# Rotary embedding in place, 32 KB rows: stores moved from SyncE's DMA ring to ScalarE's, one more load in advance

## The chip, the cores and the metric

One core of one Trainium2 chip. The metric is the device time of one execution in microseconds (us), as a median of three or more executions. The profile's span is about 1.8 us shorter than that time.

Words used below. *PE* is TensorE, *DVE* VectorE, *ACT* ScalarE, *SP* SyncE. A *DMA engine* is one of the core's 16 engines that move data; a *ring* is the queue of descriptors that one issuing engine fills, with a part on each of the 16. A *packet* is one record of the trace of a DMA engine's work. *Load n* and *store n* are the transfers of slab n, 0 to 7.

## The reference, cut to what matters

```python
# x: (16, 512, 1024) fp32; cos, sin: (512, 32) fp32; 16 heads of 64
x = x.reshape(batch, seq, num_heads, head_dim)
x1, x2 = x[..., :half_dim], x[..., half_dim:]
rotated = concatenate([x1 * cos - x2 * sin,
                       x1 * sin + x2 * cos], axis=-1)
```

33.6 MB are read and 33.6 MB written, and there is little arithmetic for each byte.

## The kernel before

A slab is two batches: 4 MB, 128 partitions with one contiguous row of 32 KB each. The slab is loaded, worked on in place in four chunks of 2,048 columns, and stored from the same tile. There are eight slabs and five slots for them. For each chunk ACT casts to bf16, DVE multiplies by the cosine and by the signed sine table, PE adds the two products (the second with its halves swapped) through an identity matrix into PSUM, and ACT copies the sum back into the slab.

```python
nb = 2; slots = 5; lead = 4; rows = 2        # W = 8192, PW = 2048 columns

def load(s):
    slab[s] = slabs.tile([P, W], f32, tag="slab", name="slab")
    nc.sync.dma_start(out=slab[s], in_=dram(x, s))

for s in range(lead):
    load(s)
# ... cos and sin are loaded in ScalarE's ring; tables are built ...
for s in range(nslabs):
    xs = slab.pop(s)
    for k in range(rpp // rows):
        # ... xb = bf16(xk); t1 = xb * cc; t2 = xb * ss; acc = t1 + swap(t2) ...
        nc.scalar.copy(out=xk, in_=acc)
    nc.sync.dma_start(out=dram(out_flat, s), in_=xs)
    if s + lead < nslabs:
        load(s + lead)
```

## Time and profile before

| | before |
|---|---|
| median time, three runs | 164.93 us (164.80 to 165.01) |
| span of the profile | 163.1 us |
| mean rate over the span | 412 GB/s |
| share of the 16 DMA engines' time, ring q1 | 96.3% |
| ACT busy | 117.3 us (72%) |

From the page of the kernel before: ACT's and the DMA's row (the span in 40 slices, busy share in tenths), then the rings with packets, MB and share of the 16 engines' time.

```profile
ACT  3006648999899999998997999999789999100000
...
DMA  6999998999999999999999999999999999999980
...
q1 hardware_dynamic: 2304, 67.11, 96.3%
q10 hardware_dynamic: 160, 0.13, 0.2%
q8 instruction: 2, 0.03, 0.1%
q14 instruction: 2, 0.02, 0.0%
HBM read 33.69 MB, written 33.55 MB: 412 GB/s over the span
```

The DMA row is full from end to end, and ACT, the busiest compute engine, stops one seventh of the span early. The stores are issued at 34.2 to 139.1 us (the view of their line):

```profile
L133 SPq DMA_DIRECT2D out_dram<-slab x8: 332/344/378, 34.2 to 139.1; - x8
```

So the DMA engines bound this kernel. All data is in q1, SyncE's ring; q10, ScalarE's, holds the two tables. The two lines called "instruction" are four small transfers that fetch the kernel's own instructions.

The next view is the last microseconds, in windows of 1 us; the columns of use here are the last two, the share of the DMA engines and GB/s. The view counts a packet in the window in which it starts, so a full window can read over 1.00, and an engine at work on one 32 KB packet (1.2 us) can show nothing.

```profile
157.00:158.00 1.00, 0.00 (x0) 0.00 (x0) 0.00 (x0) 0.00 (x0) 0.00 (x0) 0.50 1.06 459
158.00:159.00 1.00, 0.00 (x0) 0.00 (x0) 0.00 (x0) 0.00 (x0) 0.00 (x0) 0.50 0.31 131
159.00:160.00 1.00, 0.00 (x0) 0.00 (x0) 0.00 (x0) 0.00 (x0) 0.00 (x0) 0.50 0.08 33
160.00:161.00 1.00, 0.00 (x0) 0.00 (x0) 0.00 (x0) 0.00 (x0) 0.00 (x0) 0.50 0.08 33
161.00:162.00 1.00, 0.00 (x0) 0.00 (x0) 0.00 (x0) 0.00 (x0) 0.00 (x0) 0.50 0.00 0
```

A packet is 1.21 us of one engine, 1.21 / 16 = 0.076 of the 16. So 0.08 is exactly one engine: from 159 us on, single engines start a last packet while the others are done. The individual records say the same: most engines end between 158.3 and 159.4 us, two at 160.0 and 160.1, and the last at 161.8.

The chain of work that ended last, by engine, follows the compute and never names a store:

```profile
PE 28%; ACT 24%; issue 14%; DMA 10%; DVE 8%; ACTq 0%; DVEq 0%
```

### The profile page before, as it was taken

The numbers are of one execution on the slowest core, as the hardware profiler recorded it, in microseconds if no ns is written. First come the engines' busy times: TensorE is split into PE (matmuls) and PEld (weight loads), VectorE is DVE, ScalarE is ACT, GpSimd is POOL, SyncE is SP. The second block draws the span as 40 slices with busy tenths as digits, with TensorE's granted clock in tenths as the row PEclk, the third lists the DMA queues.
The fourth block names the chain that finished last, engine by engine and source line by source line (L and its number), as shares of the span: only waits on it lengthen the run. The fifth ranks groups of instructions, "written<-read, shape, count | busy, mean of one in ns | idle before, by whom it ended". The sixth has DMA issues, their size and how long they took to land.

```text
span 163.1 us, 830 instructions
## 1 busy us (share of the span) xinstructions
PE 78.8 (48%) x258; PEld 28.8 (18%) x258; DVE 76.0 (47%) x69; ACT 117.3 (72%) x65; POOL 1.1 (1%) x8
## 2 busy tenths in 40 slices
PE   0001189458918863974199419905990696000000
PEld 0000024112402320331033103301330132000000
DVE  0001699079537755871597069609920991000000
ACT  3006648999899999998997999999789999100000
POOL 2000000000000000000000000000000000000000
PEclk9999999985795997599858956995597599855555
DMA  6999998999999999999999999999999999999980
GB/s 225 426 394 402 466 434 386 466 434 402 482 402 402 498 382 410 482 396 426 450 410 444 442 410 426 450 418 442 426 426 438 426 426 450 418 450 418 434 370 16
DMA packets 2468, 67.29 MB, mean 412 GB/s; under 512 B 288, under 2 KB 416, under 8 KB 416
## 3 DMA queue, kind: packets, MB, share of 16 engines
q1 hardware_dynamic: 2304, 67.11, 96.3%
q10 hardware_dynamic: 160, 0.13, 0.2%
q8 instruction: 2, 0.03, 0.1%
q14 instruction: 2, 0.02, 0.0%
HBM read 33.69 MB, written 33.55 MB: 412 GB/s over the span
## 4 chain that ended last, share of the span: by engine, by line
PE 28%; ACT 24%; issue 14%; DMA 10%; DVE 8%; ACTq 0%; DVEq 0%
PE acc L127 15%; ACT slab L132 15%; PE acc L125 13%; DMA sin_sb<-in_sin_dram 10%; ACT xb L115 10%; DVE t L121 7%; DVE t L120 1%; PE acc L104 0%; ACTq L77 0%; DVE ss L94 0%; DVE ss L96 0%; ACTq L132 0%; DVEq L120 0%; DVE ss L106 0%; ACTq L115 0%
## 5 line engine op out<-in xcount | busy, mean ns | idle before, releaser
L125 PE MATMUL acc<-t,ident 128*128 128x512 bf16 x128 | 59.1, 462 | 34.3 <-DVE t L120 31.0
L115 ACT CAST xb<-slab 128x2048 bf16<-128x2048 f32 x32 | 59.2, 1904 | 13.0 <-DMA slab<-in_x_dram 10.4
L132 ACT COPY slab<-acc 128x2048 f32<-128x2048 f32 x32 | 58.9, 1869 | 6.9 <-PE acc L127 6.7
L127 PE MATMUL acc<-t,ident 128*128 128x512 bf16 x128 | 58.3, 455 | 6.6 <-DVE t L121 6.6
L120 DVE TENSOR_TENSOR t<-xb,cc 128x2048 bf16<-128x2048 bf16 x32 | 39.1, 1221 | 42.1 <-ACT xb L115 42.1
L121 DVE TENSOR_TENSOR t<-xb,ss 128x2048 bf16<-128x2048 bf16 x32 | 39.0, 1219 | 0.0
L127 PEld LDWEIGHTS <-ident 128*128 128x128 bf16 x128 | 14.4, 112 | 56.5 <-issue 48.5
L125 PEld LDWEIGHTS <-ident 128*128 128x128 bf16 x128 | 14.2, 111 | 38.7 <-issue 27.7
L104 PE MATMUL acc<-cc,spread 64*128 64x512 bf16 x1 | 0.6, 582 | 12.7 <-DVE cc L91 12.7
L91 DVE CAST cc<-cos_sb 64x512 bf16<-64x512 f32 x1 | 0.4, 419 | 12.3 <-DMA cos_sb<-in_cos_dram 12.3
L104 PE MATMUL acc<-ss,spread 64*128 64x512 bf16 x1 | 0.6, 583 | 4.7 <-DVE ss L96 4.7
L115 ACT ACT_TABLE_LOAD x1 | 1.3, 1283 | 1.9 <-issue 1.9
L94 DVE CAST ss<-sin_sb 64x256 bf16<-64x256 f32 x1 | 0.3, 285 | 4.8 <-DMA sin_sb<-in_sin_dram 4.8
L104 PEld LDWEIGHTS <-spread 64*128 64x128 bf16 x2 | 0.2, 102 | 12.6 <-issue 10.8
L106 DVE CAST ss<-acc 128x512 bf16<-128x512 f32 x1 | 0.7, 692 | 0.1
L106 DVE CAST cc<-acc 128x512 bf16<-128x512 f32 x1 | 0.7, 676 | 0.0
L85 POOL COPY spread<-ident 64x64 bf16<-64x64 bf16 x2 | 0.4, 230 | 0.1
masks.py:199 POOL TENSOR_SCALAR_AFFINE_SELECT ident<-ident 128x128 bf16<-128x128 bf16 x1 | 0.3, 292 | 0.1
L96 DVE TENSOR_SCALAR ss<-sin_sb 64x256 bf16<-64x256 f32 x1 | 0.3, 278 | 0.0
masks.py:197 POOL MEMSET ident<- 128x128 bf16 x1 | 0.2, 205 | 0.3 <-POOLq L152 0.3
L152 POOL MEMSET const-bfloat16-1.0<- 128x1 bf16 x1 | 0.1, 101 | 0.0
L152 POOL MEMSET const-uint8-127<- 128x1 uint8 x1 | 0.1, 101 | 0.0
(2 smaller groups left out, 0.2 us busy)
## 6 DMA issues: line engine op xcount, KB each, us to landing
slab<-in_x_dram SPq DMA_DIRECT2D x8, 4096.0 KB, 30.2
out_dram<-slab SPq DMA_DIRECT2D x8, 4096.0 KB, 28.9
cos_sb<-in_cos_dram ACTq DMA_DIRECT2D x1, 64.0 KB, 11.5
sin_sb<-in_sin_dram ACTq DMA_DIRECT2D x1, 64.0 KB, 16.2
```

The lines of the kernel that those rows point to most:

```text
L85: nc.gpsimd.tensor_copy(out=spread[:, g * SP:(g + 1) * SP], in_=ident[:SP, :SP])
L91: nc.vector.tensor_copy(out=cc1, in_=view(cos_sb, 0, (half, rpp), (0, 2), (1, half)))
L94: nc.vector.tensor_copy(out=view(ss1, 0, (hd, rpp), (1, half)), in_=sin_rows)
L96: nc.vector.tensor_scalar_mul(out=view(ss1, half, (hd, rpp), (1, half)), in0=sin_rows, scalar1=-1.0)
L104: nc.tensor.matmul(view(acc, q, (1, n)), spread, view(one, q, (1, n)), start=True, stop=True)
L106: nc.vector.tensor_copy(out=wide, in_=view(acc, 0, (1, rpp * hd)))
L115: nc.scalar.copy(out=xb, in_=xk)
L120: nc.vector.tensor_mul(out=t1, in0=xb, in1=tab(cc))
L121: nc.vector.tensor_mul(out=t2, in0=xb, in1=tab(ss))
L125: nc.tensor.matmul(bank, ident, view(t1, q, (1, BANK)), start=True, stop=False)
L127: nc.tensor.matmul(bank, ident, view(t2, q + half, (hd, hpb), (-half, 2), (1, half)), start=False, stop=True)
L132: nc.scalar.copy(out=xk, in_=acc)
```

## The change

The intent: loads in SyncE's hardware ring and stores in ScalarE's, so that the DMA engines alternate between the two by packet.

```diff
-    lead = 4
+    lead = 5
@@
-        nc.sync.dma_start(out=dram(out_flat, s), in_=xs)
+        nc.scalar.dma_start(out=dram(out_flat, s), in_=xs)
         if s + lead < nslabs:
             load(s + lead)
```

## The prediction

> **What bounds the kernel now.** The 16 DMA engines. The page's DMA row reads 9 of 10 almost throughout, and the queue section gives ring q1 96.3% of all engines' time. The trace's packet records: the 67.1 MB are 2,048 packets of 32,768 B, 128 per engine; nearly all take 1,213 ns and start as the one before ends (1,209 ns apart). 128 x 1.21 = 155 us; first packets start at 1.8 to 2.7 us; most engines end at 158.3 to 159.4 us, the slowest at 161.8; the span is 163.1. No engine idles for want of work. Compute is hidden: in the timeline ScalarE runs from 13.6 to 139.1 us, 117 us busy; the last 22 us are stores alone.
>
> **What the change does.** It removes no byte. Loads stay in SyncE's ring; stores go to ScalarE's. The Trainium skill ("DMA: Bandwidth & Descriptors", section "Queues, rings and completion order") says that each engine goes round-robin between rings by packet. The trace agrees: the cos and sin loads in ScalarE's ring, four 1 KB packets per engine each, alternate with 32 KB load packets. So a load and a store in flight each get half the rate, where now they take turns of 9.7 us.
>
> Loads 0 to 4 are queued at once instead of 0 to 3; loads 5, 6, 7 still wait for stores 0, 1, 2. I expect store 0 issued at about 34 us (as now) and done at 54 to 56 (now 52.9), and loads 5, 6, 7 to land near 87, 106 and 126 us (now 81.9, 101.4, 120.8).
>
> **The new dependence.** ScalarE's program order, compared with the one before, holds eight DMA issues, each after the next slab's first casts: store 6 stands behind two casts and a copy of slab 7, so it waits for load 7. Each issue costs ScalarE about 0.4 us (SyncE's take 0.33 to 0.40), 3 us in all, hidden. But slab 7 lands 5 us later. With casts of 1.9, two DVE products of 1.22, eight matmuls in 1.7 to 3.4 and copies of 1.87 us, I estimate store 6's issue at 134 to 136 and store 7's at 147 to 149 us (before: 139.1). A store takes 9.7 us alone, so store 7 must be issued by about 148 us or the engines run dry: the slack shrinks to nothing, costing 0 to 3 us.
>
> **A cost per switch.** By position in the slab, a load's last packet before a store takes 10 to 80 ns more on average; a store's last before a load some 10. With some 38 alternations per engine between 34 and 126 us that is an estimated 0 to 2 us. I see no gain: packets are already back to back at 27 GB/s per engine. A luckier slowest engine could give back 1 to 2 us.
>
> **Time.** 164.9 + about 1: 166.0 us, range 164.2 to 168.8. Faster by over 2%: 0.03; within 2%: 0.80; slower by over 2%: 0.17.
>
> **What would show it.** Right: about half of the DMA time each in q1 and q10, sum near 96%; packets still 1,213 to 1,250 ns; loads 5 to 7 landing 4 to 6 us later; ScalarE's last copy near 147 us; a full DMA row but for a dent near 145. Wrong: packets shorter or overlapping (gain), or longer than 1,260 ns (loss by alternation); ScalarE waiting for loads before slab 6; a hole before store 7.
>
> **What would break it.** Unfair arbitration between rings that delays load 7 or starves stores; a real cost or gain of mixing directions; PE at its lower clock in the last slab.

## The result, and the profile after

| | before | after |
|---|---|---|
| median of four runs | 164.87 us (164.68 to 165.01) | 163.49 us (163.27 to 163.78) |
| ratio | | 0.9918, 95% interval 0.9897 to 0.9939 |
| span of the profile | 163.1 us | 161.5 us |
| mean rate over the span | 412 GB/s | 416 GB/s |

A ratio is the mean time of one kernel's runs over that of the kernel before's runs of the same rounds, so it is not quite the ratio of the medians. Executions over 1.5% slower than the fastest of the same kernel are left out of the means. The change gains 0.8%, which is small and clear of the noise. The prediction forecast a loss of 1 us; the measured time lies under its range.

From the page after, the same rows:

```profile
ACT  3006647994999999899989998969990697918000
...
DMA  7999999999999999999999999999999999997996
...
q1 hardware_dynamic: 1152, 33.55, 48.9%
q10 hardware_dynamic: 1312, 33.69, 48.4%
q8 instruction: 2, 0.03, 0.1%
q14 instruction: 2, 0.02, 0.0%
HBM read 33.69 MB, written 33.55 MB: 416 GB/s over the span
```

Half of the data is in each ring. ACT now works to the end and has a hole before it; the DMA row has a dent (the 7, near 148 us). ACT's last instructions in order of time (start, duration, what, and the idle time before it with its releaser):

```profile
126.57 1.90 ACT L115 CAST xb<-slab 128x2048 bf16<-128x2048 f32 x1 [5.11 <-DMA slab<-in_x_dram]
...
134.16 0.34 ACTq L133 DMA_DIRECT2D out_dram<-slab  x1
...
145.80 3.63 ACT L132 COPY slab<-acc 128x2048 f32<-128x2048 f32 x2 [3.79 <-PE acc L127]
149.46 0.34 ACTq L133 DMA_DIRECT2D out_dram<-slab  x1
```

ACT waits 5.1 us for load 7, issues store 6 at 134.2 us and the last store at 149.5 us. This is too late to keep the DMA engines busy, as the windows of 1 us show:

```profile
147.00:148.00 1.00, 0.43 (x3) 0.00 (x0) 0.00 (x0) 1.00 (x2) 0.00 (x0) 1.00 1.14 492
148.00:149.00 1.00, 0.00 (x0) 0.00 (x0) 0.00 (x0) 1.00 (x1) 0.00 (x0) 1.00 0.23 98
149.00:150.00 1.00, 0.00 (x0) 0.00 (x0) 0.00 (x0) 0.43 (x1) 0.00 (x0) 1.00 0.08 33
150.00:151.00 1.00, 0.00 (x0) 0.00 (x0) 0.00 (x0) 0.00 (x0) 0.00 (x0) 1.00 1.22 524
...
158.00:159.00 1.00, 0.00 (x0) 0.00 (x0) 0.00 (x0) 0.00 (x0) 0.00 (x0) 0.50 1.22 524
159.00:160.00 1.00, 0.00 (x0) 0.00 (x0) 0.00 (x0) 0.00 (x0) 0.00 (x0) 0.50 0.00 0
```

Most engines sit dry from about 148.7 to 150.3 us. But the end differs from the one of before: all 16 engines start their last packet between 158 and 159 us and end within 0.2 us of each other (160.05 to 160.21 us). There is no straggler.

**Where the 1.6 us of span came from.** The completion of a transfer reaches the trace as 16 updates of a semaphore, one from each DMA engine. For each transfer take the median of the 16 and how far the last is behind it. All engines have the same work, so that lag is how late the most delayed engine is. In us, from the landing records (before a store and the next load take turns in the ring; after they share the engines):

```
            before              after
            median  last lag    median  last lag
store 0      52.82    0.18       57.17    0.12
load 4       62.20    1.37       66.87    1.41
store 1      72.28    1.08       76.54    1.38
load 5       81.67    2.16       86.26    1.37
store 2      91.69    1.87       95.94    1.53
load 6      101.17    2.75      105.62    1.41
store 3     111.14    2.48      115.30    1.50
load 7      120.54    2.83      125.00    1.49
store 6     149.66    2.82      149.26    1.47
store 7     159.32    2.83      160.46    0.09
```

The median engine ends 160.46 - 159.32 = 1.14 us *later* after the change, as the prediction said. The kernel ends with the last engine, though, and that one ends at 159.32 + 2.83 = 162.15 us before and at 160.55 us after: 1.60 us earlier, which is all of the span's difference.

The trace names no DMA engine on a packet, but packets run back to back, so each can be joined to the one that starts as it ends, which gives 16 strings of 128 data packets. (Where two packets end at the same time, the join can exchange two strings; the lags in this document are therefore read from the landing records.) In the string that ends last before the change, the events from its fetch on are:

```
 60.41 us   1,001 ns   16,384 B, instruction fetch
 61.39 us   1,720 ns   32 KB packet (the usual one takes 1,213 ns)
 80.08 us   1,765 ns   32 KB packet
 81.85 us   1,684 ns   32 KB packet
100.47 us   1,901 ns   32 KB packet
119.31 us   1,346 ns   32 KB packet
161.80 us   end of the last packet
```

The slow packets at 80 to 83, 100 to 102 and 119 us are loads, in flight while the other engines go on from a load to the store behind it in the ring (loads 5, 6 and 7 landed at medians of 81.7, 101.2 and 120.5 us). On-time engines lose something at such a point too, but less: near 60.5 us, when load 4 ended, eight other strings have a load packet of 1,292 to 1,396 ns. After the change the string that was hit by the fetch at 62.84 us has one slow packet right behind it (1,625 ns) and none over 1,330 ns later; the lag of the last engine stays near 1.4 to 1.5 us. The second fetch of 16 KB, at 123.3 us, came when load 7 was nearly done; at store 6 three engines are late, by 1.47, 1.32 and 1.09 us (before the change 2.82, 1.13 and 1.12).

### The profile page after: what moved, and what is told of

The parts are those of the page before. It is cut to its first block, busy times and chain, and to the rows that moved or that the text cites. A ratio compares the mean times of both kernels' runs of the same rounds, so it can differ in the third digit from the quotient of the medians.

```text
span 161.5 us, 816 instructions
## 1 busy us (share of the span) xinstructions
PE 79.1 (49%) x258; PEld 28.6 (18%) x258; DVE 76.4 (47%) x69; ACT 117.2 (73%) x65; POOL 1.1 (1%) x8
## 3 DMA queue, kind: packets, MB, share of 16 engines
q1 hardware_dynamic: 1152, 33.55, 48.9%
q10 hardware_dynamic: 1312, 33.69, 48.4%
## 4 chain that ended last, share of the span: by engine, by line
DMA 46%; PE 17%; ACT 14%; issue 9%; DVE 6%; ACTq 0%; DVEq 0%; SPq 0%
DMA out_dram<-slab 18%; DMA slab<-in_x_dram 18%; DMA sin_sb<-in_sin_dram 10%; PE acc L127 9%; ACT slab L132 8%; PE acc L125 7%; ACT xb L115 6%; DVE t L121 5%; DVE t L120 1%; PE acc L104 0%; ACTq L77 0%; DVE ss L94 0%; DVE ss L96 0%; DVEq L120 0%; ACTq L132 0%
```

## The experiments

**Theory A (straggler).** A fetch of instructions through a DMA engine makes that engine 1 to 1.4 us late. In a single ring, a late engine's load packets are slow when the other engines go over to a store (a *handoff*), so it falls further behind, to 2.8 us; with two rings the engines alternate by themselves, there are no such handoffs in the middle, and the lag stays.

**Theory B.** Alternating by packet is cheaper for every engine. **Theory D.** The longer lead is the gain. **Theory E.** The dry stretch before the last store is lost time, so the change gained more than 1.6 us elsewhere.

In every run the kernel before was run on the same chip; its medians there were 164.74 to 164.94 us.

### 1. The longer lead in a single ring

```diff
 # from the kernel before
-    lead = 4
+    lead = 5
```

> Theory A (straggler): the 16 KB instruction fetch near 60 us makes one DMA engine 1.4 us late, and in a single ring the late engine's last load packets before a store phase are slow, so it gets later at each load-to-store handoff after the fetch (to 2.8 us before). With a fifth load ahead and all in one ring the order becomes five loads, two stores, two loads, two stores, one load, stores: two handoffs after the fetch in place of four. A expects a last engine 1.8 to 2.3 us behind the median and 164.0 to 164.6 us. Theory B (mixing by packet itself makes every engine's packets cheaper): no change against before, 164.9, since the ring is still one. Theory D (the longer lead makes the gain): 163.5 as after.

Measured: 164.36 us, ratio 0.9975 (0.9959 to 0.9991). The order in the ring was the one expected. The last engine ended 2.61 us behind the median: its lag was 1.77 us after the fetch at 60.7 us, 1.67 at load 5, and 2.52 at load 6, with one load packet of 2,252 ns that started at 90.0 us, when the others went over to store 2. The time is in A's range, the lag 0.3 us over it. D as it was stated (163.5 us) falls. But the longer lead does give 0.25% in a single ring, about a third of the 0.8% of the change.

### 2. and 3. No PE work, in one ring and in two

```diff
-            acc = psum.tile([P, PW], f32, tag="acc")
-            # ... eight matmuls ...
-            nc.scalar.copy(out=xk, in_=acc)
+            nc.vector.tensor_add(out=t1, in0=t1, in1=<t2, halves swapped>)
+            nc.scalar.copy(out=xk, in_=t1)
```

> The PE's 512 instructions are gone (VectorE adds the two products in bf16, ScalarE copies the sum to fp32), so both 16 KB instruction fetches should be gone; one ring as before. Result should be right to bf16 rounding. A: no engine gets 1.4 us late at 60 us, so at the end the last engine is under 1.2 us behind the median (8 KB fetches may remain); the DMA ends near 160 us and the time is 162.0 to 163.3 us, at or below the change's. B: one ring still pays its switches, 164.5 to 165.

> The same kernel with the stores in ScalarE's ring and the longer lead. A: with no straggler the ring split has nothing left to save: within 0.5 us of the one-ring version without PE, if the last store is issued in time (by about 148.5 us); each microsecond later adds one. B: 1.4 us faster than the one-ring version without PE.

Measured: one ring 164.40 us (0.9971, 0.9942 to 1.0), two rings 173.02 us (1.0503). Both are right in result, and both times miss what A expected. The 16 KB fetches were gone, but two 8 KB fetches were left, and in one ring these were enough. Lag of the last and of the next to last engine at the loads and stores (medians left out):

```
             last   next
load 4       0.49   0.18
store 1      0.39   0.23    fetch of 8 KB at 67.74 us on one engine
load 5       0.94   0.63
store 2      0.64   0.29    fetch of 8 KB at 95.25 us on another
load 6       2.02   1.66
store 3      1.69   1.33
load 7       2.74   2.66
store 4      2.69   2.60
```

The lag comes up at the loads, that is, before each handoff, and not at the stores. Two engines that were 0.9 and 0.6 us late at load 5 were 2.7 us late at load 7, two handoffs on. In two rings the engine with the 8 KB fetch at 74.86 us ended store 6 just 1.04 us behind. So the growth is confirmed; wrong was that only a large fetch starts it. (The one-ring kernel too ran dry before its last store, issued at 149.0 us: the last two stores landed 10.60 us apart in place of 9.66, and the lag fell from 2.79 us at store 6 to 1.85 at the end.) The 173 us come from elsewhere: the last store was issued only at 159.1 us, since ACT waited for DVE's third operation, and the engines stood still for about 11 us (stores 6 and 7 landed 20.8 us apart in place of 9.7):

```profile
147.00:149.00 2.00, 0.00 (x0) 0.00 (x0) 2.00 (x3) 2.00 (x2) 0.00 (x0) 1.00 0.65 279
149.00:151.00 2.00, 0.00 (x0) 0.00 (x0) 2.00 (x3) 1.22 (x1) 0.00 (x0) 1.00 0.00 0
151.00:153.00 2.00, 0.00 (x0) 0.00 (x0) 2.00 (x3) 1.63 (x1) 0.00 (x0) 1.00 0.00 0
```

### 4. The last store in two halves

```diff
 # from the kernel after: the last slab is stored in two DMAs of 16 KB rows,
+            if s == nslabs - 1 and k % 2 == 1:
+                nc.scalar.dma_start(out=<half of the rows>, in_=<columns of chunks k-1, k>)
```

> The changed kernel with the last slab stored in two halves of 16 KB rows, the first about 8 us before the second, so that the engines do not run dry for 1.5 us before the last store. A: the two engines that were hit by a fetch reach the end of store 6 1.4 us behind the median, which is what the dry stretch lasted; they had no dry stretch, so the end stays: 163.2 to 163.7 us, and the median engine ends 1.4 us before the last. Rival E (the dry stretch is lost time): 162.0 to 162.3 us.

Measured: 165.66 us (163.91 to 166.13), ratio 1.0036 (0.998 to 1.0092). This did not test what it was made for. With the added DMA issue ACT's program came out in another order: the last chunk's cast stood behind a copy that waited for PE, a second copy waited once more, and the second half was issued 7 us later than the whole store of the changed kernel. ACT's last two copies and the issue, in order of time:

```profile
145.52 1.87 ACT L132 COPY slab<-acc 128x2048 f32<-128x2048 f32 x1 [5.68 <-PE acc L127]
...
154.47 1.87 ACT L132 COPY slab<-acc 128x2048 f32<-128x2048 f32 x1 [5.29 <-PE acc L127]
156.37 0.34 ACTq L136 DMA_DIRECT2D out_dram<-slab  x1
```

### 5. Stores of 16 KB rows, so that loads get two thirds

```diff
 # from the kernel after
-        nc.scalar.dma_start(out=dram(out_flat, s), in_=xs)
+        for h in range(2):
+            nc.scalar.dma_start(out=<half h of the rows>, in_=<half h of the columns>)
```

> The changed kernel with each store in two of 16 KB rows, so that one 32 KB load packet alternates with one 16 KB store packet and loads get two thirds of the rate while both rings have work. Load 7 should land near 118 us (126.5 in the changed kernel) and the last store be issued well before the engines run dry: no dry stretch. A: the end is then the most-delayed engine's, 1.1 to 1.8 us behind the median: 163.0 to 163.8 us. E (the dry stretch of the changed kernel is lost time): 161.9 to 162.4.

Measured: 164.80 us (164.21 to 166.24), ratio 1.0004 (0.9953 to 1.0056). The dry stretch was gone (last store issued at 146.3 us, median engine done at 159.27 us, 1.2 us before that of the changed kernel), and still the kernel was slower than the changed one: the last engine was 2.45 us behind. E's time (161.9 to 162.4 us) is missed: a kernel without the dry stretch was not faster. But its lag was larger than the changed kernel's as well, so this run does not separate the two. A's figures for the lag (1.1 to 1.8 us) and the time (163.0 to 163.8) missed, and load 7 landed at 122.2 us, not near 118. The lag moved up and down on the way, up to 3.9 us; where it grew was not followed up.

### 6. One ring, with the handoffs put together

```diff
 # from the kernel before, with lead = 5
-        if s + lead < nslabs:
-            load(s + lead)
+        if s == 2:
+            for n in range(lead, nslabs):
+                load(n)
```

> One ring, five loads, then three stores, three loads, five stores: one load-to-store handoff after the fetch near 60 us (at about 111 us) in place of four. A: the hit engine is 1.4 to 1.8 us late after the fetch and gains at most one step more at 111 us: last engine 1.5 to 2.6 us behind the median, 163.7 to 164.5 us. If rings alone matter (B): 164.9.

Measured: 164.00 us, ratio 0.9934 (0.991 to 0.9958). The lag was 1.69 us after the fetch at 60.7 us and 1.66 us as far as load 6, through two stores and two loads without a handoff. It went to 2.18 us at load 7, with one load packet of 1,896 ns at 109.4 us, just before the only handoff, and ended at 2.28 us. So a single ring gains most of what two rings gain if it has fewer handoffs. B falls: one ring alone does not make 164.9.

### 7. and 8. Half slabs, mixed and not mixed

```diff
 # loads and stores in two DMAs each, rows of 16 KB; the mixed order is
+        for h in range(2):
+            nc.sync.dma_start(out=<store half h of slab s>)
+            nc.sync.dma_start(<load half h of slab s + lead>)
 # the control has both store halves, then both load halves
```

> One ring, half slabs of 16 KB rows; store and load halves take turns, so that there are twice as many handoffs from load to store between 60 and 121 us (eight in place of four). A: the late engine loses at each; last engine 3.5 to 5 us behind the median, 1 us or more slower than the same halves not mixed. B: the finer mixing helps or does nothing: equal or faster than the unmixed halves.

> The control: one ring, half slabs of 16 KB rows, both halves of a store before both halves of the next load, so the handoffs are those of the kernel before. A: last engine 2.3 to 3 us behind the median, 164.7 to 165.6 us (as before, plus what the smaller packets cost).

Measured: mixed 171.14 us, with two of its four runs and the profile slow; its two fast runs are 169.14 and 169.97 us, ratio 1.028 (1.0246 to 1.0314). Control 165.79 us, ratio 1.0054. The mixed one is slower, but not for A's reason. Its last engine was 3.34 us behind before its last two half stores (in the profiled run, a slow one), the control's 3.25 us before its last half store (1.64 after the fetch, then 2.69, then slowly to 3.25). So the control missed its own expectation a little as well, in lag (2.3 to 3 us) and in time (up to 165.6), and it stood dry for about 2.1 us before its last half store, issued at 155.7 us. Twice the handoffs did not make twice the lag: the growth levels off near 3 us. The mixed kernel lost its time in dry stretches before its last two half stores, the last of which was issued at about 163 us; that too is read from the slow run, and no fast run was profiled. A's expectation of 3.5 to 5 us failed, and lag per handoff is not a constant.

### 9. and 10. No fetch at all: ScalarE alone, wrong result

```diff
-    rows = 2
+    rows = 4
@@ each chunk, result wrong on purpose
             nc.scalar.copy(out=xb, in_=xk)
-            # ... DVE and PE work ...
-            nc.scalar.copy(out=xk, in_=acc)
+            nc.scalar.copy(out=xk, in_=xb)
```

> Wrong result on purpose: each chunk is only cast to bf16 and copied back by ScalarE (tiles of 4,096 columns), so there are too few instructions for any fetch during the run; the ring, the loads and the stores are those of the kernel before. A: without a fetch no engine gets late, so the four handoffs after 60 us cost nothing: last engine under 0.7 us behind the median, time 161.5 to 162.6 us although the ring is one. B (the single ring itself costs): 164 to 165.

> The same wrong-result kernel with the stores in ScalarE's ring and the longer lead. A: ties with the one-ring version within 0.5 us, as there is no late engine to protect. B: 1.4 us faster than it.

Measured: one ring 162.54 us, ratio 0.9866 (0.9841 to 0.9892); two rings 164.27 us, ratio 0.997 (0.9949 to 0.9991). No instruction was fetched in either after the start. In one ring the last engine ended 0.79 us behind the median, and the kernel was faster than the changed one although its ring is single and has all its handoffs. A's time is met, at the upper end of its range; its lag (under 0.7 us) is missed by 0.1. With two rings it did not tie, as A had said, but lost 1.7 us. Here the dry stretches did cost time, because no engine was late enough to use them (at store 5 the last was 0.45 us behind): store 6 and store 7 were issued so late that the engines stood still twice, for about 1.4 and 1.0 us. The median engine ended 2.09 us later than with one ring, the last one 1.38 us.

```profile
138.00:139.00 1.00, 0.00 (x0) 0.00 (x0) 0.00 (x0) 1.00 (x1) 0.00 (x0) 1.00 0.45 197
139.00:140.00 1.00, 0.00 (x0) 0.00 (x0) 0.00 (x0) 1.00 (x2) 0.00 (x0) 1.00 0.01 0
...
149.00:150.00 1.00, 0.00 (x0) 0.00 (x0) 0.00 (x0) 1.00 (x1) 0.00 (x0) 1.00 0.38 164
150.00:151.00 1.00, 0.00 (x0) 0.00 (x0) 0.00 (x0) 0.16 (x1) 0.00 (x0) 1.00 0.01 0
```

### 11. The changed kernel without its dry stretch

```diff
 # from the kernel after; the last slab's result is wrong on purpose
             nc.scalar.copy(out=xb, in_=xk)
+            if s == nslabs - 1:
+                nc.scalar.copy(out=xk, in_=xb)
+                continue
```

> The changed kernel with a wrong result on purpose: the last slab skips VectorE and PE, so its store is issued near 142 us in place of 149.5 and the engines do not run dry. Everything before is the same, both 16 KB fetches included. A: the median engine ends 1.3 us earlier (near 158.9), but the engine that a fetch made 1.4 us late now ends last, near 160.2: 163.0 to 163.6 us, no faster than the changed kernel. E (the dry stretch is lost time): 161.9 to 162.4 us.

Measured: 163.76 us (163.28 to 164.16), ratio 0.994 (0.991 to 0.997). The last store was issued at 144.6 us; windows of 1 us:

```profile
149.00:150.00 1.00, 0.00 (x0) 0.00 (x0) 0.00 (x0) 0.00 (x0) 0.00 (x0) 0.50 0.84 360
...
158.00:159.00 1.00, 0.00 (x0) 0.00 (x0) 0.00 (x0) 0.00 (x0) 0.00 (x0) 0.50 0.16 66
159.00:160.00 1.00, 0.00 (x0) 0.00 (x0) 0.00 (x0) 0.00 (x0) 0.00 (x0) 0.50 0.08 33
```

The dry stretch is gone (the first line read 0.08 after the change), the median engine ends at 158.86 us, 1.6 us earlier than in the changed kernel, and the time is not shorter: E's time is missed for the second time, and A's (163.0 to 163.6 us) by 0.2. The straggler is back: it ended 2.46 us behind. So again the larger lag hides what the dry stretch was worth; with the changed kernel's lag of 1.47 us this kernel would have ended near 158.86 + 1.47 = 160.33 us, an estimate, 0.2 us before the changed one. A had 1.4 us for it; the same engine had also met a load packet of 2,107 ns at 37.3 us, when store 0 began, 28 us before its fetch. That start is the one handoff that two rings keep. In the changed kernel eight engines had slow load packets there too, but of 1,341 to 1,438 ns.

### 12. A first attempt at a better kernel

```diff
 # two rings, DVE adds the products in place (no PE work), tiles of 4,096 columns
-    rows = 2
+    rows = 4
+            nc.vector.tensor_mul(out=t2, in0=xb, in1=tab(ss))
+            nc.vector.tensor_mul(out=xb, in0=xb, in1=tab(cc))
+            nc.vector.tensor_add(out=xb, in0=xb, in1=<t2, halves swapped>)
```

> An attempt at a better correct kernel: two rings, VectorE adds the products (no PE work), tiles of 4,096 columns, so that almost nothing is fetched during the run. A: no late engine; if the last store is issued by 148.5 us, 161.8 to 162.6 us; each microsecond later adds one. B: no better than the changed kernel, 163.5.

Measured: right in result, 192.62 us, ratio 1.1701. ACT's program had the casts of several chunks in a row and then their copies, so that DVE and ACT waited for each other; the last store was issued at 178.5 us. It tells nothing of the theories.

### 13. and 14. Few instructions, the work kept, one ring and two

Open after 12 runs was whether the missing fetches or the missing work made the ScalarE-only kernel fast. These two are correct and do all the work. They are kernel 12 with the next chunk's cast written ahead of the chunk's own operations, so that ACT alternates between casts and copies:

```diff
+    do_cast(0)
+    for n, (s, k) in enumerate(steps):
+        do_cast(n + 1)
         # ... DVE: t2, xb * cc, xb + swapped t2 ...
         nc.scalar.copy(out=xk_of(s, k), in_=xb)
 # one ring: five loads, three stores, three loads, five stores, all by SyncE
 # two rings: loads by SyncE, stores by ScalarE, as in the changed kernel
```

> Correct result with full work, one ring: five loads, three stores, three loads, five stores; VectorE adds the products, tiles of 4,096 columns, each chunk's cast ahead of the chunk before's copy, so hardly any instruction is fetched before the last store is issued (near 140 us). A: no engine gets late; last engine under 0.8 us behind the median, 162.0 to 162.7 us, faster than the changed kernel. If the missing work was what made the ScalarE-only kernel fast: 163.5 to 165.

> The same work and few instructions, stores in ScalarE's ring, loads as in the changed kernel. A: no late engine, so the time is set by when the last store is issued: load 7 lands near 126 us and ScalarE and VectorE need 21 us more; issue at 147.5 to 149 us, a dry stretch of 0 to 1 us, 162.2 to 163.2 us: not faster than one ring. If two rings save something of their own (B): 1 us or more faster than the one-ring kernel of this call.

Measured: one ring 162.70 us (162.24 to 162.74), ratio 0.9867 (0.985 to 0.9883); two rings 162.69 us (162.43 to 162.97), ratio 0.9878 (0.9862 to 0.9894). The rings on the page of the one-ring kernel,

```profile
q1 hardware_dynamic: 2304, 67.11, 97.6%
q10 hardware_dynamic: 160, 0.13, 0.2%
q14 instruction: 1, 0.01, 0.0%
HBM read 33.69 MB, written 33.55 MB: 419 GB/s over the span
```

and the windows of 1 us at its end:

```profile
157.00:158.00 1.00, 0.00 (x0) 0.00 (x0) 0.00 (x0) 0.00 (x0) 0.00 (x0) 1.00 1.21 524
158.00:159.00 1.00, 0.00 (x0) 0.00 (x0) 0.00 (x0) 0.00 (x0) 0.00 (x0) 1.00 0.01 0
```

One fetch of 8 KB was left in each, at 123.3 and 119.7 us, so late that there was no handoff, or next to none, to come: the last engine ended 0.60 and 0.74 us behind. Neither kernel has a dry stretch (the last store lands 9.6 to 9.7 us after store 6, as in the kernel before). One ring and two rings tie, as A said. Both beat the kernel before by 1.2 to 1.3%, and their medians are 0.8 us under the changed kernel's; the two were not run side by side with it.

### Summary of the lag

| kernel | median time, us | time of the profiled run, us | last engine behind the median at store 6, us | dry before the last store |
|---|---|---|---|---|
| before: one ring | 164.87 | 164.91 | 2.82 | no |
| after: two rings | 163.49 | 163.32 | 1.47 | yes |
| one ring, longer lead (1) | 164.36 | 164.34 | 2.60 | no |
| one ring, no PE work (2) | 164.40 | 164.64 | 2.79 | yes |
| two rings, stores of 16 KB rows (5) | 164.80 | 164.49 | 2.47 | no |
| one ring, few handoffs (6) | 164.00 | 164.02 | 2.26 | no |
| two rings, no dry stretch (11) | 163.76 | 164.16 | 2.49 | no |
| one ring, ScalarE only (9, wrong result) | 162.54 | 162.67 | 0.77 | no |
| one ring, few instructions (13) | 162.70 | 162.24 | 0.61 | no |
| two rings, few instructions (14) | 162.69 | 162.43 | 0.75 | no |

In one and the same run, the time follows the lag: the time of the profiled run less its lag is 161.6 to 162.1 us in every row, whatever the rings, also in the two rows whose dry stretch was about as short as their lag or shorter. The medians follow it more roughly, since other runs of a kernel have other lags (run 11). Left out are runs 3, 4, 7, 10 and 12, which stood dry for longer than their lag, and run 8, whose loads too are of 16 KB rows.

## Why the prediction was wrong

- **What bounds the kernel: right.** The DMA engines do, with equal work and back-to-back packets. The prediction even read the slowest engine's end, 161.8 us, against 158.3 to 159.4 us for most.
- **The schedule: right within 1.3 us.** Loads 5, 6 and 7 landed at 87.6, 107.0 and 126.5 us (forecast 87, 106, 126), store 6 was issued at 134.2 us (134 to 136), the last store at 149.5 us (147 to 149). Store 0 was done at 57.3 us (54 to 56). The two rings took 48.9% and 48.4%.
- **The round-robin by packet: right.** The Trainium skill says it in "DMA: Bandwidth & Descriptors", section "Queues, rings and completion order". In the trace a 4 MB load and a 4 MB store in flight together each take about 19.4 us (loads 5, 6 and 7 land 19.4 us apart), twice the 9.7 us of one alone.
- **The cost per switch, "an estimated 0 to 2 us": wrong, none shows.** In the mixed stretch packets start 1,209 to 1,210 ns apart, as in the single ring (1,215 where a semaphore is written). The 10 to 80 ns per handoff were real as an average over 16 engines; but from load 5 on most of it sat on one or two late engines, at 130 to 690 ns on a packet of the last one, and they came from the single ring. To multiply the average by the number of alternations turned a cost of the old kernel into one of the new.
- **"The slack shrinks to nothing, costing 0 to 3 us": right in mechanism, wrong in what it costs.** The dry stretch was there (the last two stores land 11.20 us apart in place of 9.66, so 1.54 us), and the median engine did end 1.14 us later. But the engine that was late used the others' dry stretch to catch up. Without it, the last engine would have ended near 149.26 + 1.47 + 9.66 = 160.39 us; it ended at 160.55. So it cost 0.16 us, an estimate from this one run. Runs 5 and 11, which have no dry stretch, are not faster, though they do not settle it alone, as their last engines ended 2.45 and 2.46 us behind.
- **The step that failed: the slowest engine's term.** The prediction wrote "A luckier slowest engine could give back 1 to 2 us", called it luck, and its sum stayed a loss of about 1 us. It was the gain: the lag at store 6 went from 2.82 to 1.47 us, 1.35 us less. (The rest of the 1.60 us: at store 6 the median engine is 0.40 us earlier, at 149.26 in place of 149.66 us, less the 0.16 of the dry stretch. Those 0.40 us need no alternating between rings: in one ring, runs 1 and 6 have 149.30 and 149.32 us.) It has a cause in the change. Run 1 differs from the changed kernel in the ring alone and has a lag of 2.60 us. Runs 1, 2 and 6 show that a late engine gets later at handoffs in a single ring, and runs 9, 13 and 14 that where no fetch comes before the last handoffs a single ring is as fast as two or faster. Part of it is chance as well: in run 11 two rings had a lag of 2.49 us, 0.9 us of it from the one handoff they keep. The four runs of the changed kernel all lie within 0.5 us, but only one was examined by packets.

What stays open: why a load packet takes 1.4 to 2.2 us while the other engines begin a store, when it takes 1.21 us among loads and stores that have been alternating for a while; why the lag levels off near 3 us; and what decides which DMA engine a fetch falls on.

## What to carry to other kernels

A kernel bound by DMA ends when the last of its 16 engines ends, so read the spread of the engines at the end and not the mean share: here 2.8 us of 163 lay in one engine, and two rings, fewer handoffs or fewer instructions each took a part of it away. In these runs two rings do not move data faster than one (162.69 and 162.70 us when no engine is late); they keep a late engine from getting later, and they pay with later loads, which turn into a dry stretch before the last store. Transfers that are 0.1% of the bytes, such as instruction fetches, can cost 1%: one fetch on one engine was enough to start its lag.

## What the Trainium skill lacked or had wrong

- "Runtime: NRT & Kernel Launch", section "Instruction fetch mechanics", says that instructions are refilled in 16 KiB blocks through the sequencer's own DMA queue and that the cost is mostly hidden. The runs agree on the block for one queue (16,384 B at 60.4 and 122.4 us in the kernel before); in another the fetches are of 8,192 B (72.5 and 87.1 us), which the section does not have. What is missing is the cost to the data: a fetch of 16 KB takes one of the 16 DMA engines for 0.9 to 1.1 us, the 32 KB packet behind it takes 1.58 to 1.72 us in place of 1.21, and in the kernel before this engine ended 2.8 us behind the median. Correct kernels with few instructions ran in 162.7 us against 164.8.
- "DMA: Bandwidth & Descriptors", section "Rules for kernel authors", says that spreading DMAs over several issuing engines for bandwidth does not help. The runs agree: 419 GB/s over the span and 162.70 and 162.69 us with one ring and with two, when nothing is late. What is missing: with a late engine the choice of ring does matter (lag of 2.82 us against 1.47), through load-to-store handoffs in a single ring, at which a late engine's load packets took 1.35 to 2.25 us.
- The same page, section "Queues, rings and completion order", gives a packet as about 9 to 17 descriptors. Here each 32,768 B row is one packet in the records, and the rings alternate in steps of that size (how many descriptors a row is, the trace does not tell); with 16 KB rows in the store ring the loads went ahead faster (loads 3 and 4 landed 14.5 us apart in place of 19.4). None of its sections says that the row size sets the share of each ring.
